# A tuned decoder layer on one core: one of the four weight-block sums of each gate/up group moves from VectorE to GpSimd

## The chip, the core and the metric

The kernel runs on one core of a Trainium2 chip. The core's engines each have an instruction queue of their own and work in parallel: TensorE (PE in the profile; its weight loads are PEld), VectorE (DVE), ScalarE (ACT), GpSimd (POOL) and SyncE (SP), which here only starts DMA transfers. An engine takes its queue strictly in order; semaphores tie the queues together. The metric is the device time of one execution in microseconds (us); the kernel before takes 2040.13 us, the median of two runs (2040.05 and 2040.21).

## The reference, cut to what matters

One decoder layer on 256 tokens of width 2048, all in float32. It has a SwiGLU feed-forward half-step, a token mixer of two attention branches, and a second SwiGLU half-step, each followed by a LayerNorm:

```python
def _swiglu(x, w_gate, w_up, w_down):
    return (jax.nn.silu(x @ w_gate) * (x @ w_up)) @ w_down

h = _layer_norm(ALPHA * h + 0.5 * _swiglu(h, ffn1_w_gate, ffn1_w_up, ffn1_w_down), ln1_g, ln1_b)
mix = _mixer(h, ...)
h = _layer_norm(ALPHA * h + mix, ln2_g, ln2_b)
h = _layer_norm(ALPHA * h + 0.5 * _swiglu(h, ffn2_w_gate, ffn2_w_up, ffn2_w_down), ln3_g, ln3_b)
```

Here x is 256 x 2048, and w_gate and w_up are each 2048 x 5632. The change touches only the products x @ w_gate and x @ w_up of the two half-steps.

## The kernel before, in words

**Products in three parts.** A float32 product is made of three TensorE products in the type fp32r. Every operand is split into a high part (a rounding cast on ScalarE, line 149) and a low part (operand minus high part, a two-input subtract on VectorE, line 150). `triple` issues high x high, high x low and low x high (lines 202, 203, 204); line 203 is the first to read the low part of a weight tile.

**The ring.** Weights come from memory in pieces of 128 x 1024 floats (512 KB), which SyncE fetches. The two halves of a split piece go into a pair of `wring` tiles; in this stage six pairs are used in turn. A piece is one unit of work: its load is issued, some units later its `prep` makes the split, some units later still `now` issues its matmuls. A pair is free again when TensorE has done with it, so ScalarE's cast for a later unit waits for TensorE when the ring is full.

**Groups.** The gate and up weights are laid out in chunks of 512 columns (256 gate, 256 up). The first two chunks of a half-step go the plain way (`project`). The other twenty are taken two by two: ten groups per half-step, 20 in all. In a group (`Hybrid.group`) the upper half of the depth is multiplied plainly (eight `plain` units of 12 matmuls, whose tiles are called `raw`), and the lower half by a scheme with seven block products in place of eight (`seventh`; 14 units of 6 matmuls, with activations called `xs`). The scheme multiplies sums of weight blocks. There are four blocks, "11", "12", "21" and "22", each of two pieces (s = 0 and 1), in eight fixed tiles called `sraw`: 451 and 452 hold block 11, 453 and 454 block 12, 455 and 456 block 21, 457 and 458 block 22, in the first half-step. Products 5, 6, 7 and 4 need a sum, made in place by VectorE in `prep` (line 316) just ahead of the split: for product 5 block 11 += block 12, for product 6 block 11 += block 22, for product 7 block 12 += block 22, for product 4 block 11 += block 21. That is eight adds of 128 x 1024 in a group and 160 in all. The products stand in the order 1, 5, 6, 7, 2, 4, 3, with a plain unit behind each.

**Other work of a group.** When a bank of sums is complete, VectorE adds a stored product (line 504) and multiplies gate and up (line 495), ScalarE applies the SiLU (line 491), VectorE transposes 32 x 32 blocks (line 483), and GpSimd starts eight DMAs that write the result to memory (line 485). These DMA starts are all that GpSimd does in the groups.

**What sets the order.** The program is not issued in the order of the code: a scheduler places every instruction into its engine's queue when the kernel is built. So an edit in one place can shift neighbours on other queues.

Of the kernel before, what the change touches and what calls it, by code (L numbers as in the profile page):

```python
# [15 lines left out]
ALU = mybir.AluOpType  # L16
# [43 lines left out]
def layer_kernel(ctx: ExitStack, tc: tile.TileContext, a: dict, out: bass.AP):  # L60
    nc = tc.nc
    V, S, GP, PE = nc.vector, nc.scalar, nc.gpsimd, nc.tensor
# [9 lines left out]
    def nm(s):  # L72
        uid[0] += 1
        return f"{s}_{uid[0]}"
# [10 lines left out]
    def mm_bank(name="mm"):  # L85
        return psum.tile([P, 512], F32, tag="mm", name=nm(name), bufs=5)
# [61 lines left out]
    def split(hi, lo, src):  # L148
        S.copy(hi, src)  # L149
        V.tensor_tensor(out=lo, in0=src, in1=hi.bitcast(F32), op=ALU.subtract)  # L150
# [12 lines left out]
    def catch_up(n):  # L163
        while len(behind) > n:
            behind.popleft()()
# [22 lines left out]
    def unit(load, prep, now, later_on=None):  # L188
        if load is not None:
            load()  # L190
        loaded.append((prep, now, later_on))
        advance(*ahead)

    def next_pair():
        assert len(ring) > len(prepared) + lag[0], (len(ring), len(prepared), lag[0])
        catch_up(len(ring) - 1)
        pair = ring.pop(0)
        ring.append(pair)
        return pair

    def triple(o, xh, xl, wh, wl, first, last, again=False):
        PE.matmul(o, xh, wh, start=first, stop=False, skip_group_check=again)  # L202
        PE.matmul(o, xh, wl, start=False, stop=False, skip_group_check=again)  # L203
        PE.matmul(o, xl, wh, start=False, stop=last, skip_group_check=again)  # L204
# [68 lines left out]
    class Hybrid:  # L273
# [8 lines left out]
        def group(self, w0, w1, done):  # L282
            banks = {}
            snap = [t[:, i, :] for t in self.snaps[self.turn % 2] for i in range(2)]
            self.turn += 1
            n1, n2, n3, q5 = snap
            R = self.raws
            blocks = {"11": (w0, 0), "12": (w1, 0), "21": (w0, 2), "22": (w1, 2)}

            plan = {1: ("11", "11", None, "X"), 5: ("12", "11", ("11", "12"), "Z"), 6: ("22", "11", ("11", "22"), "X"),  # L290
                    7: (None, "12", ("12", "22"), "X"), 2: ("21", "21", None, "Y"), 4: (None, "11", ("11", "21"), "W"),
                    3: (None, "22", None, "Z")}
            after = {1: lambda: S.copy(n1, banks["X"]), 6: lambda: S.copy(n2, banks["X"]),  # L293
                     7: lambda: S.copy(n3, banks["X"]), 5: lambda: S.copy(q5, banks["Z"]),
                     2: lambda: done(0, 0, banks["Y"], n1, ALU.subtract),
                     4: lambda: done(0, 1, banks["W"], n3, ALU.subtract)}
            stops = {1, 5, 6, 7, 2, 4}

            def bank(n):
                first = n not in banks  # L300
                if first:
                    banks[n] = mm_bank()
                return banks[n], first

            def seventh(p, s):
                load_block, src, add, b = plan[p]
                st = {}

                def load():
                    w, j0 = blocks[load_block]  # L310
                    nc.sync.dma_start(R[load_block][s], w[j0 + s])

                def prep():
                    t = R[src][s]
                    if add is not None:
                        V.tensor_tensor(out=t, in0=t, in1=R[add[1]][s], op=ALU.add)  # L316
                    pair = next_pair()
                    split(*pair, t)
                    st["pair"] = [v.rearrange("p (g n) -> p g n", g=G) for v in pair]

                def now():
                    o, first = bank(b)
                    wh, wl = st["pair"]
                    xh, xl = self.seven.at_[p]
                    for g in range(G):
                        k = 2 * s + g
                        triple(o, xh[:, k, :], xl[:, k, :], wh[:, g, :], wl[:, g, :], first and g == 0,
                               s == 1 and g == 1 and p in stops, b in "XZ")
                    if s == 1 and p in after:
                        after[p]()  # L330
                unit(load if load_block else None, prep, now)

            def plain(n, j, last=False):
                w = (w0, w1)[n]
                names = (("Y", "W"), ("Z", "X"))[n]
                st = {}

                def load():
                    st["raw"] = wpool.tile([P, 1024], F32, tag="raw", name=nm("raw"), bufs=4)
                    nc.sync.dma_start(st["raw"], w[j])  # L340

                def prep():
                    pair = next_pair()
                    split(*pair, st["raw"])
                    st["pair"] = [v.rearrange("p (g n) -> p g n", g=G) for v in pair]

                def now():
                    wh, wl = st["pair"]
                    for b in range(2):
                        o, first = bank(names[b])  # L350
                        for g in range(G):
                            k = 2 * j + g
                            triple(o, self.x.at(0, k, b), self.x.at(1, k, b), wh[:, g, :], wl[:, g, :],
                                   first and g == 0, last and g == 1, n == 1)
                    if last:
                        done(1, 0, banks["Z"], n2, ALU.add)
                        done(1, 1, banks["X"], q5, ALU.add)
                unit(load, prep, now)

            end = self.k_tiles // G - 1  # L360
            for p, n, j in ((1, 0, 4), (5, 0, 5), (6, 0, 6), (7, 0, 7), (2, 1, 4), (4, 1, 5), (3, 1, 6)):
                for s in range(2):
                    seventh(p, s)
                plain(n, j)
            plain(1, end, True)
# [642 lines left out]
```

## Time and profile before

| what | value |
|---|---|
| time, median of two runs | 2040.13 us |
| span of the profiled execution, first to last instruction | 2038.9 us |
| PE busy | 2016.2 us (99%) |
| DVE busy | 1513.5 us (74%) |
| ACT busy | 1153.0 us (57%) |
| POOL busy | 147.4 us (7%) |
| block sums on DVE (line 316) | 160, together 192.5 us, 1215 ns each |
| mean granted TensorE clock | 0.997 |

The profile gives no total of its own for its execution beside the span; the span is 1.2 us below the median of the runs. "Busy" is a share of the whole span, and the stages differ: the groups of the first half-step fill about 60 to 480 us of the span and those of the second about 1340 to 1790 us, and there VectorE is far busier than its 74%. A matmul's end is modelled, so a busy TensorE is best read by how many matmuls start in a stretch.

### The profile page before, as it was taken

How to read it: one execution, taken by the hardware profiler on the slowest of the kernel's cores; microseconds unless marked ns; L12 is line 12 of the kernel's file. 1: busy time of each engine (PE TensorE's matmuls, PEld its weight loads, DVE VectorE, ACT ScalarE, POOL GpSimd, SP SyncE). 2: the span in 40 equal slices, each digit the busy share in tenths (PEclk: the TensorE clock that was granted, in tenths of full speed). 3: DMA queues.
4: the chain of work that ended last, by engine and by line, in shares of the span. 5: the costliest groups of instructions: out<-in, count | busy, mean ns of one | idle time of the engine just before them, and what ended most of it. 6: DMA issues, size and time to landing. Idle time of an engine off the chain costs nothing.

```text
span 2038.9 us, 25040 instructions
## 1 busy us (share of the span) xinstructions
PE 2016.2 (99%) x9088; PEld 1668.6 (82%) x9088; DVE 1513.5 (74%) x1765; ACT 1153.0 (57%) x1443; POOL 147.4 (7%) x279
## 2 busy tenths in 40 slices
PE   8999999999999999999999999999999999999997
PEld 7788888887888888888888888878888888878886
DVE  6999999997545675455665555699999999965545
ACT  5666666675333565554674445476666666753332
POOL 0110001022000000000000000001000110220000
PEclk9999999999999999999999999999999999999999
DMA  7766766677655755544555575666676667785664
GB/s 268 250 202 221 247 217 196 217 274 272 203 193 192 237 183 199 171 150 155 166 170 192 187 277 187 214 230 222 215 238 227 198 214 237 246 290 193 196 194 136
DMA packets 123675, 432.15 MB, mean 212 GB/s; under 512 B 16464, under 2 KB 16544, under 8 KB 123552
## 3 DMA queue, kind: packets, MB, share of 16 engines
q1 hardware_dynamic: 108000, 387.50, 56.9%
q0 software_dynamic: 14400, 40.96, 6.4%
q10 hardware_dynamic: 1152, 2.10, 0.3%
q8 instruction: 71, 1.16, 0.2%
q14 instruction: 52, 0.43, 0.1%
HBM read 412.66 MB, written 17.83 MB: 211 GB/s over the span
## 4 chain that ended last, share of the span: by engine, by line
PE 90%; DVE 4%; DMA 3%; issue 3%; ACT 0%; POOL 0%; DVEq 0%; SPq 0%; ACTq 0%; POOLq 0%
PE mm L203 29%; PE mm L204 29%; PE mm L202 29%; DVE wring L150 2%; DMA sraw<-in_gu_dram 1%; DMA hraw<-hT 1%; DMA xraw<-in_xT_dram 1%; PE tr L370 1%; DVE sraw L316 1%; PE tr L652 0%; DMA raw<-in_gu_dram 0%; ACT wring L149 0%; PE tr L767 0%; PE tr L796 0%; PE tr L765 0%
## 5 line engine op out<-in xcount | busy, mean ns | idle before, releaser
L150 DVE TENSOR_TENSOR wring<-raw,wring 128x1024 fp32r<-128x1024 f32 (+1 forms) x582 | 702.7, 1210 | 433.5 <-ACT wring L149 428.7
L149 ACT CAST wring<-raw 128x1024 fp32r<-128x1024 f32 (+1 forms) x582 | 605.3, 1043 | 570.1 <-PE mm L204 489.0
L202 PE MATMUL mm<-wring,h 128*128 128x512 f32 (+2 forms) x1632 | 635.0, 389 | 1.6 <-ACT h L149 1.6
L204 PE MATMUL mm<-wring,h 128*128 128x512 f32 (+2 forms) x1632 | 630.3, 387 | 0.6 <-DVE h L150 0.6
L203 PE MATMUL mm<-wring,h 128*128 128x512 f32 (+2 forms) x1632 | 629.5, 386 | 0.8 <-DVE wring L150 0.8
L204 PEld LDWEIGHTS mm<-wring,h 128*128 128x128 f32 x1632 | 306.4, 188 | 63.7 <-DVE h L150 2.5
L202 PEld LDWEIGHTS mm<-wring,h 128*128 128x128 f32 x1632 | 306.6, 188 | 63.5 <-ACT h L149 3.4
L203 PEld LDWEIGHTS mm<-wring,h 128*128 128x128 f32 x1632 | 306.7, 188 | 61.9 <-DVE wring L150 2.1
L149 ACT CAST wring<-sraw 128x1024 fp32r<-128x1024 f32 x280 | 289.9, 1052 | 115.5 <-PE mm L204 74.6
L150 DVE TENSOR_TENSOR wring<-sraw,wring 128x1024 fp32r<-128x1024 f32 x280 | 335.7, 1219 | 9.3 <-ACT wring L149 6.8
L202 PE MATMUL mm<-wring,xs 128*128 128x512 f32 x560 | 218.0, 389 | 2.1 <-ACT snap L293 2.1
L203 PE MATMUL mm<-wring,xs 128*128 128x512 f32 x560 | 218.0, 389 | 0.5 <-DVE wring L150 0.5
L204 PE MATMUL mm<-wring,xs 128*128 128x512 f32 x560 | 217.9, 389 | 0.0
L316 DVE TENSOR_TENSOR sraw<-sraw,sraw 128x1024 f32<-128x1024 f32 x160 | 192.5, 1215 | 1.7 <-DMA sraw<-in_gu_dram 1.4
L202 PE MATMUL mm<-wring,x 128*128 128x512 f32 x384 | 149.6, 391 | 4.1 <-ACT x L149 4.1
L203 PE MATMUL mm<-wring,x 128*128 128x512 f32 x384 | 149.9, 391 | 0.8 <-DVE wring L150 0.8
L204 PE MATMUL mm<-wring,x 128*128 128x512 f32 x384 | 149.8, 391 | 0.0
L485 POOL DMA_DIRECT2D hT<-blocks x176 | 95.5, 550 | 665.6 <-DVE blocks L483 662.9
L202 PEld LDWEIGHTS mm<-wring,xs 128*128 128x128 f32 x560 | 105.1, 188 | 24.5 <-ACT snap L293 2.5
L203 PEld LDWEIGHTS mm<-wring,xs 128*128 128x128 f32 x560 | 105.1, 188 | 22.7 <-DVE wring L150 0.9
L204 PEld LDWEIGHTS mm<-wring,xs 128*128 128x128 f32 x560 | 105.1, 188 | 21.7
L202 PEld LDWEIGHTS mm<-wring,x 128*128 128x128 f32 x384 | 72.2, 188 | 19.9 <-ACT x L149 4.5
(239 smaller groups left out, 1543.1 us busy)
## 6 DMA issues: line engine op xcount, KB each, us to landing
raw<-in_gu_dram SPq DMA_DIRECT2D x192, 512.0 KB, 4.4
raw<-in_dn_dram SPq DMA_DIRECT2D x176, 512.0 KB, 3.4
sraw<-in_gu_dram SPq DMA_DIRECT2D x160, 512.0 KB, 5.3
raw<-in_wgm_dram SPq DMA_DIRECT2D x32, 512.0 KB, 3.4
raw<-in_wgd_dram SPq DMA_DIRECT2D x32, 512.0 KB, 3.3
raw<-in_w_out_dram SPq DMA_DIRECT2D x32, 512.0 KB, 3.5
hT<-blocks POOLq DMA_DIRECT2D x176, 64.0 KB, 2.5
hraw<-hT POOLq DMA_DIRECT2D x44, 256.0 KB, 5.0
```

The source lines that it names most:

```text
L149: S.copy(hi, src)
L150: V.tensor_tensor(out=lo, in0=src, in1=hi.bitcast(F32), op=ALU.subtract)
L202: PE.matmul(o, xh, wh, start=first, stop=False, skip_group_check=again)
L203: PE.matmul(o, xh, wl, start=False, stop=False, skip_group_check=again)
L204: PE.matmul(o, xl, wh, start=False, stop=last, skip_group_check=again)
L316: V.tensor_tensor(out=t, in0=t, in1=R[add[1]][s], op=ALU.add)
L370: PE.transpose(t[:, i * P:(i + 1) * P], src[:, i * P:(i + 1) * P], ident)
L485: nc.gpsimd.dma_start(hT[q, b].rearrange("(g r) (i f) -> i r g f", g=4, i=4)[i], t[32 * i:32 * (i + 1), :].rearrange("r (g f) -> r g f", g=4))
```

## The change

The two adds of product 7 (block 12 += block 22, s = 0 and 1) leave VectorE. GpSimd makes them, and they are issued in `prep` of product 6, beside the VectorE add of blocks 11 and 22, three units before the split that needs them. The arithmetic is the same. In each group VectorE has six adds of 128 x 1024 left and GpSimd gets two; over the kernel 40 adds move.

```diff
@@ -312,8 +312,10 @@
                 def prep():
                     t = R[src][s]
-                    if add is not None:
+                    if add is not None and p != 7:
                         V.tensor_tensor(out=t, in0=t, in1=R[add[1]][s], op=ALU.add)
+                    if p == 6:
+                        GP.tensor_tensor(out=R["12"][s], in0=R["12"][s], in1=R["22"][s], op=ALU.add)
                     pair = next_pair()
                     split(*pair, t)
```

Lines behind the edit have numbers higher by two in the changed kernel. The scheduler's order changes with it, shown here for the fifth and sixth groups of the first half-step.

VectorE's queue ahead of the transposes, before; `sraw_453` is block 12, piece 0:

```order
L316 TENSOR_TENSOR sraw_452<-sraw_452,sraw_454 128x1024
L150 TENSOR_TENSOR wring_107<-sraw_451,wring_106 128x1024
L316 TENSOR_TENSOR sraw_453<-sraw_453,sraw_457 128x1024
L504 TENSOR_TENSOR gus_2038<-mm_1804,snap_459 128x512
L150 TENSOR_TENSOR wring_125<-sraw_452,wring_124 128x1024
```

The same place now:

```order
L316 TENSOR_TENSOR sraw_452<-sraw_452,sraw_454 128x1024
L150 TENSOR_TENSOR wring_107<-sraw_451,wring_106 128x1024
L316 TENSOR_TENSOR sraw_451<-sraw_451,sraw_457 128x1024
L506 TENSOR_TENSOR gus_2038<-mm_1806,snap_459 128x512
L150 TENSOR_TENSOR wring_125<-sraw_452,wring_124 128x1024
```

The add of block 12's first piece is gone, and product 6's first add (block 11) has moved up into its place.

VectorE's queue behind the two transposes, before; it holds the splits of product 6 (`sraw_451`, `sraw_452`) and product 7 (`sraw_453`, `sraw_454`):

```order
L316 TENSOR_TENSOR sraw_451<-sraw_451,sraw_457 128x1024
L316 TENSOR_TENSOR sraw_452<-sraw_452,sraw_458 128x1024
L150 TENSOR_TENSOR wring_109<-raw_2071,wring_108 128x1024
L150 TENSOR_TENSOR wring_121<-sraw_451,wring_120 128x1024
L150 TENSOR_TENSOR wring_119<-sraw_452,wring_118 128x1024
L150 TENSOR_TENSOR wring_107<-sraw_453,wring_106 128x1024
L316 TENSOR_TENSOR sraw_454<-sraw_454,sraw_458 128x1024
L150 TENSOR_TENSOR wring_123<-raw_2109,wring_122 128x1024
L150 TENSOR_TENSOR wring_121<-sraw_455,wring_120 128x1024
L150 TENSOR_TENSOR wring_125<-sraw_454,wring_124 128x1024
```

The same place now:

```order
L150 TENSOR_TENSOR wring_121<-sraw_451,wring_120 128x1024
L316 TENSOR_TENSOR sraw_452<-sraw_452,sraw_458 128x1024
L150 TENSOR_TENSOR wring_109<-raw_2071,wring_108 128x1024
L316 TENSOR_TENSOR sraw_451<-sraw_451,sraw_455 128x1024
L150 TENSOR_TENSOR wring_119<-sraw_452,wring_118 128x1024
L150 TENSOR_TENSOR wring_107<-sraw_453,wring_106 128x1024
L150 TENSOR_TENSOR wring_125<-sraw_454,wring_124 128x1024
L150 TENSOR_TENSOR wring_123<-raw_2111,wring_122 128x1024
L150 TENSOR_TENSOR wring_121<-sraw_455,wring_120 128x1024
```

The add of block 12's second piece is gone; product 6's second split is still the fifth instruction behind the transposes, since product 4's first add (block 11 += block 21) has moved up ahead of it.

GpSimd's queue in this place now; before, it held only the line 485 rows:

```order
L318 TENSOR_TENSOR sraw_453<-sraw_453,sraw_457 128x1024
L318 TENSOR_TENSOR sraw_454<-sraw_454,sraw_458 128x1024
L487 DMA hT_132<-blocks_2059 32x4x128 x4
L487 DMA hT_132<-blocks_2065 32x4x128 x4
L318 TENSOR_TENSOR sraw_453<-sraw_453,sraw_457 128x1024
L318 TENSOR_TENSOR sraw_454<-sraw_454,sraw_458 128x1024
```

Each pair of adds stands ahead of the eight DMA starts that write the previous group's result.

## The prediction

> **What bounds the kernel now.** I read the page's busy times and its chain of waits first, then the table by stretch of time, then who waits for whom in the groups. First the two lines of the page, then two rows of the table by stretch:
>
> ```profile
> PE 2016.2 (99%) x9088; PEld 1668.6 (82%) x9088; DVE 1513.5 (74%) x1765; ACT 1153.0 (57%) x1443; POOL 147.4 (7%) x279
> PE 90%; DVE 4%; DMA 3%; issue 3%; ACT 0%; POOL 0%; DVEq 0%; SPq 0%; ACTq 0%; POOLq 0%
> ...
> core 0: us, PE busy (x) PEld busy (x) DVE busy (x) ACT busy (x) POOL busy (x), PEclk, DMA share, GB/s
> 270.30:311.10 40.80, 40.80 (x182) 33.80 (x181) 39.56 (x41) 26.38 (x30) 4.33 (x9) 1.00 0.66 219
> 1427.00:1467.80 40.80, 40.80 (x182) 33.78 (x181) 39.55 (x41) 26.38 (x32) 4.33 (x9) 1.00 0.67 219
> ```
>
> The chain is 90% TensorE. The two long rows are one group of each half-step. A group has 8 x 12 + 14 x 6 = 180 matmuls, and 40.8 us over 180 is 0.227 us each, at full clock and without a pause. Beside it VectorE is busy 39.56 of 40.8 us, so it has 1.2 us to spare in a group. TensorE binds, and VectorE follows close behind.
>
> ```profile
> PE mm L202 <- ACT snap L293: 2.1, 1, 2.1
> PE mm L204 <- DVE h L150: 0.6, 1, 0.6
> PE mm L203 <- DVE wring L150: 0.5, 1, 0.5
> PE mm L202 <- ACT h L149: 0.3, 1, 0.3
> ```
>
> These are all of TensorE's waits from 55 to 500 us (total, times, longest). The same view of 1310 to 1790 us has no row. So TensorE loses 3.5 us in the groups and around them, and nothing that is taken from VectorE there can bring more than that.
>
> How far is VectorE ahead of TensorE? The next fence shows one group's stretch: VectorE's timeline, then ScalarE's, then TensorE's (start, length, engine, line; in brackets the idle time before).
>
> ```profile
> 258.15 1.22 DVE L316 TENSOR_TENSOR sraw<-sraw,sraw 128x1024 f32<-128x1024 f32 x1
> ...
> 261.56 1.21 DVE L316 TENSOR_TENSOR sraw<-sraw,sraw 128x1024 f32<-128x1024 f32 x1
> 262.70 1.22 DVE L150 TENSOR_TENSOR wring<-sraw,wring 128x1024 fp32r<-128x1024 f32 x1
> 263.83 1.21 DVE L316 TENSOR_TENSOR sraw<-sraw,sraw 128x1024 f32<-128x1024 f32 x1
> 264.97 0.68 DVE L504 TENSOR_TENSOR gus<-mm,snap 128x512 f32<-128x512 f32 x1
> ...
> 269.11 1.30 DVE L483 STREAM_TRANSPOSE blocks<-hb 128x512 f32<-128x512 f32 x2
> 270.33 2.31 DVE L316 TENSOR_TENSOR sraw<-sraw,sraw 128x1024 f32<-128x1024 f32 x2
> 272.62 1.23 DVE L150 TENSOR_TENSOR wring<-raw,wring 128x1024 fp32r<-128x1024 f32 x1
> 273.76 3.49 DVE L150 TENSOR_TENSOR wring<-sraw,wring 128x1024 fp32r<-128x1024 f32 x3
> 277.17 1.22 DVE L316 TENSOR_TENSOR sraw<-sraw,sraw 128x1024 f32<-128x1024 f32 x1
> ...
> 263.37 1.05 ACT L149 CAST wring<-sraw 128x1024 fp32r<-128x1024 f32 x1 [1.67 <-PE mm L204]
> 271.53 1.06 ACT L149 CAST wring<-raw 128x1024 fp32r<-128x1024 f32 x1 [2.18 <-PE mm L204]
> 274.87 1.05 ACT L149 CAST wring<-sraw 128x1024 fp32r<-128x1024 f32 x1
> ...
> 276.96 0.39 PE L203 MATMUL mm<-wring,xs 128*128 128x512 f32 x1
> 278.32 0.39 PE L203 MATMUL mm<-wring,xs 128*128 128x512 f32 x1
> ```
>
> ScalarE's cast at 263.37 had waited 1.67 us for TensorE: the ring was full, and nothing could have been prepared earlier. From there VectorE works without a gap through adds, bank sums, transposes and splits, and its lead shrinks. The row at 273.76 holds three splits: product 6, pieces 0 and 1, and product 7, piece 0. Three in 3.49 us, each 1.22 long, start (3.49 - 1.22) / 2 = 1.14 us apart, so the second ends at 273.76 + 1.14 + 1.22 = 276.1. TensorE first reads its low part at 278.32. That is a lead of 2.2 us, the end of a burst, and it comes back in every group. **The cover over VectorE in this place is 2.2 us**, though it is idle 1.2 us per group elsewhere: idle time behind a full ring cannot be saved up.
>
> **The change part by part.**
>
> *What VectorE loses.* Two adds per group. Adds start 1.13 or 1.14 us after the instruction before (262.70 to 263.83, 263.83 to 264.97), so two are worth 2.3 us per group and 46 us over the 20. TensorE was not waiting for them, so by itself this gives between 0 and 3.5 us. I take 0.
>
> *Where it is lost.* The add at 263.83 (block 12, piece 0) goes, and product 6's first add takes its place. The one at 277.17 (piece 1) goes from behind the tight split. Ahead of that split stand as many VectorE instructions as before, because block 11 += block 21 has moved up. So the lead of 2.2 us there is not made larger by the saving.
>
> *What GpSimd gets.* Two adds of 128 x 1024, two tiles in, one out. Before has no such add; these are its nearest rows, three from GpSimd's groups by shape (count, then busy us and mean ns) and one from its timeline.
>
> ```profile
> L584 POOL TENSOR_SCALAR_AFFINE_SELECT mask<-mask 128x128 f32<-128x128 f32 x2 | 0.5, 287 | 0.0
> L582 POOL MEMSET mask<- 128x384 f32 x1 | 0.4, 422 | 0.0
> ...
> L992 POOL MEMSET const-float32-0.0<- 128x1 f32 x1 | 0.1, 98 | 0.2 <-issue 0.2
> ...
> 270.10 4.33 POOL L485 DMA_DIRECT2D hT<-blocks  x8 [36.47 <-DVE blocks L483]
> ```
>
> One element costs 98 ns, so 98 ns is the fixed part. A fill of 384 takes 422: (422 - 98) / 384 = 0.84 ns per element for one stream. The select reads one tile and writes one: (287 - 98) / 128 = 1.48 ns. An add has one more stream to read. Low: two streams at fill speed, 1024 x 1.69 + 98 = 1.83 us. Middle: select plus one stream, 1024 x 2.32 + 98 = 2.47 us. High: two selects, 1024 x 2.95 + 98 = 3.12 us. I take 2.3 us, near the middle.
>
> *Is GpSimd in time?* Its first add needs only the VectorE add of blocks 11 and 12 to be over (258.15 + 1.22 = 259.4), the second the one at 261.56 (262.8); block 22 has landed, since the add at 263.83 ran without a gap. The first user is the cast of block 12 at 274.87. Two adds of 2.3 us are done by about 265 to 267. They stand ahead of the eight DMA starts, which began at 270.10 when the transposes released them; these wait for nothing new, and what they write is read only at the end of the half-step. GpSimd has 36.47 us of idle time there, so the add's own length is hidden.
>
> *What the add does to VectorE.* This decides, and no row shows it: before never has GpSimd reading tiles beside VectorE. The bounds for the time that VectorE stands still per add are 0 and the whole add (3.12 us). The nearest row speaks for little: beside the DMA starts at 270.10 VectorE's adds run at (272.62 - 270.33) / 2 = 1.145 us instead of 1.135. But a DMA start reads no tile, and both the add and the VectorE instructions beside it stream two. I choose the upper kind, a VectorE that stands still for the whole add, 2.3 us.
>
> [...]
>
> *The sum.* Both adds fall between 259.4 and the tight split. VectorE reaches that split 2 x 2.3 = 4.6 us later, 2.2 of them are covered, and TensorE waits 2.4 us. Behind it VectorE has time enough (1.2 + 2.3 us saved) to fill the ring again by the next burst; so the loss comes anew in every group: 20 x 2.4 = 48 us. The profiled span of 2038.9 becomes 2087, and with the 1.2 us by which the median stands above it, **2088 us**, 2.3% slower. In short, with B for the standstill per add: loss = 20 x (2B - 2.2). B = 1.83 gives 29 us (2069), 3.12 gives 81 (2121), B up to 1.1 gives none.
>
> [...]
>
> *Small things.* ScalarE's queue gets one more table load near the first group. A table load takes 1.28 us in this row:
>
> ```profile
> 80.83 1.28 ACT L630 ACT_TABLE_LOAD   x1
> ```
>
> That is once, and it is the most it can cost. SyncE's loads keep their number; a few change places at the start of each half-step, for which I allow 2 us either way.
>
> **The rivals.**
>
> *The engines do not hold each other (0.26).* VectorE simply does 2.3 us less per group, TensorE keeps its 0.227 us per matmul, and the time is 2040 less 0 to 3.5 us: about 2038, not slower. The spacing of 1.145 us beside the DMA starts speaks for it. It decides whenever B stays below 1.1 us, since the lead of 2.2 us then covers both adds.
>
> *GpSimd only gets in where VectorE leaves room (0.18).* If VectorE's back-to-back instructions keep the add waiting, it starts at one that does not read two such tiles, as at 264.97 (0.6 us to the next), and VectorE stands still for 2.3 - 0.6 = 1.7 us: 20 x (3.4 - 2.2) = 24 us, 2064. If both go on at half pace, B is about 1.15 and the loss 2 us. So 2040 to 2064.
>
> *GpSimd comes too late (0.02).* If its adds wait so long that the second ends past the cast at 274.87, product 7's split is late too, and each microsecond costs another 20 us: above 2104.
>
> That the scheduler undoes the change can be excluded: the adds stand in GpSimd's queue, and VectorE's queue has two fewer.
>
> **How the numbers follow.** A measurement here can tell about 2%, 41 us; the mark is 2081, which is B = 2.13. The standstill for a whole add has 0.54: 0.46 with B above 2.13, 0.08 with a shorter add (2069 to 2081). The forecast is 2088. The range must take in the rival without contention, 2036, and at the top B = 2.7, 2104; outside lie longer adds and late ones, under 0.2. Slower by over 2%: 0.46 + 0.02 = 0.48. Within 2%: 0.08 + 0.18 + 0.26 = 0.52, less 0.01. Faster by over 2%: 0.01, since TensorE's waits leave 3.5 us to gain.
>
> **What would show it.** GpSimd has 40 adds, 2.3 us each. VectorE's spacing in those moments grows from 1.14 to over 3 us. TensorE gets waits for line 150, about 2.4 us per group, and a group grows from 40.8 to 43.2 us. Under the first rival the groups stay at 40.8 us and VectorE's busy time falls to about 37.3. Wrong in its core would be a group that stays at 40.8 us while VectorE stands still, or one that grows with GpSimd's adds late and VectorE free.

## The result and the profile after

The changed kernel takes 2112.75 us (median of two runs, 2110.06 and 2115.44) against 2040.13 us: a ratio of 1.0351, 95% interval 1.0333 to 1.0368, so 3.5% slower. The forecast was 2088 us and its range ended at 2104. The direction was right; of some 72 us the sum had 48. The profiled execution has a span of 2108.3 us, 69.4 us more than before, and a mean granted TensorE clock of 0.984 against 0.997.

The page of the changed kernel (lines below 318 have moved down by two) shows the moved work: busy times, chain, and the groups of the adds.

```profile
PE 2049.8 (97%) x9088; PEld 1684.0 (80%) x9088; DVE 1554.1 (74%) x1725; ACT 1146.8 (54%) x1444; POOL 281.5 (13%) x319
PE 86%; DVE 6%; issue 4%; DMA 3%; POOL 1%; ACT 1%; DVEq 0%; ACTq 0%; SPq 0%; POOLq 0%
...
L318 POOL TENSOR_TENSOR sraw<-sraw,sraw 128x1024 f32<-128x1024 f32 x40 | 134.1, 3352 | 542.7 <-DVE sraw L316 491.3
L316 DVE TENSOR_TENSOR sraw<-sraw,sraw 128x1024 f32<-128x1024 f32 x120 | 186.3, 1554 | 3.6 <-DMA sraw<-in_gu_dram 2.9
```

GpSimd has the 40 adds. VectorE has 40 instructions fewer, but is busy for 41 us more: its remaining adds last 1554 ns in the mean and not 1215 as before. The place to look at first is one group of the first half-step, in the timelines of GpSimd and VectorE (start, length, engine, line; in brackets the idle time before).

```profile
273.55 3.31 POOL L318 TENSOR_TENSOR sraw<-sraw,sraw 128x1024 f32<-128x1024 f32 x1 [25.34 <-DVE sraw L316]
279.16 3.31 POOL L318 TENSOR_TENSOR sraw<-sraw,sraw 128x1024 f32<-128x1024 f32 x1 [2.30 <-DVE sraw L316]
288.61 4.33 POOL L487 DMA_DIRECT2D hT<-blocks  x8 [6.14 <-DVE blocks L485]
```

```profile
273.39 1.22 DVE L150 TENSOR_TENSOR wring<-sraw,wring 128x1024 fp32r<-128x1024 f32 x1
274.52 3.42 DVE L150 TENSOR_TENSOR wring<-raw,wring 128x1024 fp32r<-128x1024 f32 x1
277.87 1.21 DVE L316 TENSOR_TENSOR sraw<-sraw,sraw 128x1024 f32<-128x1024 f32 x1
279.01 1.21 DVE L150 TENSOR_TENSOR wring<-sraw,wring 128x1024 fp32r<-128x1024 f32 x1
280.25 3.30 DVE L316 TENSOR_TENSOR sraw<-sraw,sraw 128x1024 f32<-128x1024 f32 x1
283.48 0.68 DVE L506 TENSOR_TENSOR gus<-mm,snap 128x512 f32<-128x512 f32 x1
```

Beside each of the two GpSimd adds exactly one VectorE instruction is long: 3.42 and 3.30 us in place of 1.22. So it is in the whole trace: 40 of VectorE's two-input instructions last over 1.6 us, one for each add (34 of them 3.3 to 3.4 us, the others 2.8 to 3.2); in the trace of the kernel before there is none. Start to start it is 277.87 - 274.52 = 3.35 and 283.48 - 280.25 = 3.23 us; without the add it would be 1.14. So VectorE stands still for **2.21 and 2.09 us**, 4.3 us in a group. GpSimd's own 3.31 us holds both a wait and the work: its first add is recorded from 273.55, but VectorE's split of 273.39 still ends in time (274.61); the work lies behind that, 276.86 - 274.61 = 2.25 us.

What TensorE makes of it is in its timeline, at product 6, second piece:

```profile
292.30 0.50 PE L202 MATMUL mm<-wring,xs 128*128 128x512 f32 x1
294.61 0.50 PE L203 MATMUL mm<-wring,xs 128*128 128x512 f32 x1 [1.81 <-DVE wring L150]
...
295.63 0.63 PE L203 MATMUL mm<-wring,xs 128*128 128x512 f32 x1
296.06 0.63 PE L204 MATMUL mm<-wring,xs 128*128 128x512 f32 x1
296.49 0.63 PE L202 MATMUL mm<-wring,x 128*128 128x512 f32 x1
...
298.59 0.40 PE L204 MATMUL mm<-wring,x 128*128 128x512 f32 x1
298.82 0.40 PE L202 MATMUL mm<-wring,x 128*128 128x512 f32 x1
```

There are two losses. The first is a pause: line 203 starts 2.31 us after line 202, not 0.23, because line 150 of VectorE is late. The second was not in the forecast: from 295.2 to 298.6 the matmuls start 0.43 us apart and not 0.23. The table by stretch (length; busy time of PE, PEld, DVE, ACT, POOL with counts; granted clock, DMA share, GB/s) shows the whole group and those moments:

```profile
289.40:334.10 44.70, 42.88 (x182) 34.81 (x181) 41.70 (x39) 25.93 (x30) 10.92 (x11) 0.96 0.60 202
...
296.00:297.00 1.00, 1.00 (x4) 0.74 (x3) 1.00 (x2) 0.28 (x1) 0.00 (x0) 0.50 0.02 8
297.00:298.00 1.00, 1.00 (x4) 0.80 (x3) 1.00 (x2) 1.00 (x2) 0.00 (x0) 0.50 0.92 270
298.00:299.00 1.00, 1.00 (x4) 0.79 (x4) 1.00 (x1) 0.25 (x1) 0.00 (x0) 0.73 0.88 295
299.00:300.00 1.00, 1.00 (x6) 0.80 (x6) 1.00 (x2) 0.00 (x0) 0.00 (x0) 1.00 0.87 324
```

A group that took 40.8 us takes 44.7 here, at a mean clock of 0.96, and behind the pause TensorE is granted **half its clock** for about three microseconds. TensorE's waits in the whole span are led by one row: total, times, longest.

```profile
PE mm L203 <- DVE wring L150: 37.4, 23, 2.3
```

Before, that row had 2.1 us. So some 35 of the 69 us are booked as waits for line 150; the rest had to be found.

### The profile page after: what moved, and what is told of

It is laid out like the page before. It is cut to its first block, busy times and chain, and to the rows that moved or that the text cites. A ratio compares the mean times of both kernels' runs of the same rounds, so it can differ in the third digit from the quotient of the medians.

```text
span 2108.3 us, 25175 instructions
## 1 busy us (share of the span) xinstructions
PE 2049.8 (97%) x9088; PEld 1684.0 (80%) x9088; DVE 1554.1 (74%) x1725; ACT 1146.8 (54%) x1444; POOL 281.5 (13%) x319
## 4 chain that ended last, share of the span: by engine, by line
PE 86%; DVE 6%; issue 4%; DMA 3%; POOL 1%; ACT 1%; DVEq 0%; ACTq 0%; SPq 0%; POOLq 0%
PE mm L203 28%; PE mm L204 28%; PE mm L202 27%; DVE wring L150 3%; DVE sraw L316 2%; DMA hraw<-hT 1%; DMA xraw<-in_xT_dram 1%; PE tr L372 1%; POOL hT L487 1%; ACT wring L149 0%; DMA sraw<-in_gu_dram 0%; PE tr L654 0%; DMA z<-res 0%; DMA row_i<-in_pos_row_dram 0%; DVE gus L506 0%
## 5 line engine op out<-in xcount | busy, mean ns | idle before, releaser
L150 DVE TENSOR_TENSOR wring<-raw,wring 128x1024 fp32r<-128x1024 f32 (+1 forms) x582 | 743.7, 1280 | 453.6 <-ACT wring L149 448.2
L203 PE MATMUL mm<-wring,xs 128*128 128x512 f32 x560 | 224.8, 401 | 36.0 <-DVE wring L150 36.0
L202 PE MATMUL mm<-wring,xs 128*128 128x512 f32 x560 | 222.6, 397 | 2.8 <-ACT snap L293 2.1
L204 PE MATMUL mm<-wring,xs 128*128 128x512 f32 x560 | 223.3, 399 | 0.0
L318 POOL TENSOR_TENSOR sraw<-sraw,sraw 128x1024 f32<-128x1024 f32 x40 | 134.1, 3352 | 542.7 <-DVE sraw L316 491.3
L316 DVE TENSOR_TENSOR sraw<-sraw,sraw 128x1024 f32<-128x1024 f32 x120 | 186.3, 1554 | 3.6 <-DMA sraw<-in_gu_dram 2.9
L203 PEld LDWEIGHTS mm<-wring,xs 128*128 128x128 f32 x560 | 106.9, 191 | 64.4 <-DVE wring L150 42.6
L202 PE MATMUL mm<-wring,x 128*128 128x512 f32 x384 | 153.0, 400 | 4.1 <-ACT x L149 4.1
L203 PE MATMUL mm<-wring,x 128*128 128x512 f32 x384 | 152.7, 399 | 0.8 <-DVE wring L150 0.8
L204 PE MATMUL mm<-wring,x 128*128 128x512 f32 x384 | 152.0, 397 | 0.0
L202 PEld LDWEIGHTS mm<-wring,xs 128*128 128x128 f32 x560 | 106.2, 190 | 31.6 <-ACT wring L149 7.6
L204 PEld LDWEIGHTS mm<-wring,xs 128*128 128x128 f32 x560 | 107.7, 192 | 21.7
```

Source lines behind the costliest of these rows:

```text
L318: GP.tensor_tensor(out=R["12"][s], in0=R["12"][s], in1=R["22"][s], op=ALU.add)
```

## The experiments

The theory after the first look had two parts: a GpSimd add that reads tiles holds VectorE for its whole length (2.2 us), and the pause of TensorE that follows makes its clock fall. The rivals were that the new order of VectorE's and SyncE's queues costs something by itself; that the tiles or the writes are what collide; and that the clock falls for another reason (GpSimd's activity, or simply more of everything). Edits are shown against the changed kernel.

### The new order without GpSimd's add: drop

The GpSimd add is left out, so product 7 is computed without its sum.

```diff
-                    if p == 6:
-                        GP.tensor_tensor(out=R["12"][s], in0=R["12"][s], in1=R["22"][s], op=ALU.add)
```

> Product 7 goes without its sum: neither VectorE nor GpSimd makes the 40 adds (a part of the computation is left out), and VectorE's queue is the one of the changed kernel. Theory of the standstill (GpSimd's add keeps VectorE's two-input instructions waiting): with no add on GpSimd nothing stands still, groups of 40.8 us, TensorE without waits, about 2037 us (2040 less 0 to 3.5). Rival, the new order of VectorE's queue is what costs: the loss of 70 us stays, about 2110.

Measured: 2038.68 us (2036.97 to 2039.59), ratio 0.9989 (0.9979 to 0.9998). One group by stretch:

```profile
267.70:308.50 40.80, 40.80 (x182) 33.80 (x181) 37.43 (x39) 26.43 (x30) 4.34 (x8) 1.00 0.67 219
```

VectorE is busy for 37.43 us where it was 39.56, and the group still takes 40.80. VectorE's instructions stand in the order of the changed kernel, so the reordering costs nothing, and the saving on VectorE is worth 0.1%: so much the change would bring if GpSimd's adds cost nothing.

### One add of the two: one

```diff
-                    if add is not None and p != 7:
+                    if add is not None and (p != 7 or s == 1):
...
-                    if p == 6:
+                    if p == 6 and s == 0:
```

> GpSimd adds only piece 0 of block 12, VectorE keeps piece 1. Theory of the standstill behind a lead: VectorE stands still once per group, 2.2 us, and the lead of 2.0 to 2.2 us at product 6's splits covers it: a wait of TensorE of 0 to 0.2 us, 2040 to 2048. Rival, a loss in proportion to the adds that moved: half of 72 us, about 2076.

Measured: 2052.67 us (2050.96 to 2055.67), ratio 1.0062 (1.0047 to 1.0077). VectorE has one long instruction per group, and TensorE's row for line 150 is small:

```profile
264.54 3.42 DVE L150 TENSOR_TENSOR wring<-raw,wring 128x1024 fp32r<-128x1024 f32 x1
267.88 1.21 DVE L316 TENSOR_TENSOR sraw<-sraw,sraw 128x1024 f32<-128x1024 f32 x1
```

```profile
PE mm L203 <- DVE wring L150: 4.8, 10, 1.0
```

The hold is 267.88 - 264.54 - 1.14 = 2.2 us, as much as TensorE's lead of 2.0 to 2.2, and the group grows only by 0.37 us (41.17). Half of the adds cost 12.5 of 72 us. So the loss is not proportional to the adds: the lead pays for the first, the second goes straight to TensorE. That is what the term with the lead says. The time is still 5 us above the expected 2048: the groups account for 20 x 0.37 = 7.4 us, and the trace has two windows of half clock more than before (one at 20 us, one at 78 us; their price, up to 1.6 us each, is worked out below). The last 2 us were not followed.

### Which part of the add holds VectorE: copy and memset

In copy, GpSimd copies block 22 over block 12 (one tile in, one out); in memset it fills the tile three times (none in, one out). Both leave product 7's sum out.

```diff
-                        GP.tensor_tensor(out=R["12"][s], in0=R["12"][s], in1=R["22"][s], op=ALU.add)
+                        GP.tensor_copy(R["12"][s], R["22"][s])
```

```diff
-                        GP.tensor_tensor(out=R["12"][s], in0=R["12"][s], in1=R["22"][s], op=ALU.add)
+                        for _ in range(3):
+                            GP.memset(R["12"][s], 0.01)
```

> In place of each add GpSimd copies block 22's piece over block 12's (one tile read, one written; the sum is left out). If reading one tile is enough to hold VectorE: a standstill of the copy's length, which by the select and fill rows is 1.0 to 1.6 us per piece, seen as VectorE instructions of 2.2 to 2.8 us; twice that against the lead of 2.2 gives a TensorE wait of 0 to 1 us per group, with the slower clock behind it 2037 to 2090. If it takes two read streams: VectorE stays at 1.22 us each, about 2037.

> In place of each of GpSimd's adds stand three fills of the same tile (they write and read nothing; the sum is left out). By the fill rows of before a fill of 1024 takes 0.96 us, three 2.9 us, longer than the add held VectorE (2.2 us). Theory that only GpSimd's reading of tiles holds VectorE: no standstill, VectorE keeps its spacing of 1.14 us, groups of 40.8 us, about 2037. Rival, any GpSimd access to the tiles holds it: 2.9 us per piece, more than in the changed kernel, over 2120.

Measured: copy 2041.12 us (2039.82 to 2041.63), ratio 1.0003 (0.9993 to 1.0012); memset 2038.58 us (2037.23 to 2040.98), ratio 0.9992 (0.9982 to 1.0001). First copy's timelines, GpSimd then VectorE:

```profile
259.46 1.98 POOL L318 COPY sraw<-sraw 128x1024 f32<-128x1024 f32 x1 [24.12 <-DVE sraw L316]
...
260.45 2.06 DVE L150 TENSOR_TENSOR wring<-raw,wring 128x1024 fp32r<-128x1024 f32 x1
262.43 1.21 DVE L316 TENSOR_TENSOR sraw<-sraw,sraw 128x1024 f32<-128x1024 f32 x1
```

VectorE's instruction beside the copy takes 262.43 - 260.45 = 1.98 us start to start, a hold of 0.84. Two of them are 1.7 us, less than the lead of 2.2, and TensorE sees nothing. Now memset, GpSimd then VectorE:

```profile
257.53 2.99 POOL L319 MEMSET sraw<- 128x1024 f32 x3 [25.66 <-DVE sraw L316]
...
257.39 1.22 DVE L150 TENSOR_TENSOR wring<-sraw,wring 128x1024 fp32r<-128x1024 f32 x1
258.52 1.22 DVE L150 TENSOR_TENSOR wring<-raw,wring 128x1024 fp32r<-128x1024 f32 x1
259.66 1.22 DVE L316 TENSOR_TENSOR sraw<-sraw,sraw 128x1024 f32<-128x1024 f32 x1
```

Here GpSimd writes for 3 us beside three VectorE instructions of two inputs, and each has its usual 1.22 us; in the whole trace, with 120 fills, no two-input instruction of VectorE lasts over 1.6 us. The instructions of VectorE have the same order in both runs as in the changed kernel. So in these runs GpSimd's reading holds VectorE (0.84 us beside the copy, which reads one tile, 2.1 to 2.2 beside the add, which reads two), and its writing alone does not (0 beside the fills).

### Spare work in the pause, with and without the change: fill_after and fill_before

Nine spare matmuls of 512 columns (2.0 us) go ahead of product 6's second piece, into the place of TensorE's pause; their result is not used. fill_after is the changed kernel with them, fill_before the kernel before.

```diff
                 def now():
...
+                    if p == 6 and s == 1:
+                        spare = tr_bank()
+                        for _ in range(9):
+                            PE.matmul(spare, xh[:, 2, :], wh[:, 0, :], start=True, stop=True)
```

> The changed kernel with nine added matmuls of 512 columns per group on TensorE, ahead of product 6's second piece, where TensorE waits; their result is used by nothing. If the lower clock behind the wait comes from TensorE's idle time: the nine take 2.04 us, about as long as the wait, TensorE does not fall idle, the clock stays at 1.0, and a group takes 40.8 + 2.1 = 42.9 us: about 2084, faster than the changed kernel by 28 although it does more. If the clock drops for another reason (GpSimd's work, say), they come on top or change nothing: 2112 to 2150.

> The kernel before with the same nine added matmuls per group. TensorE was never waiting there: 180 matmuls of 2.04 us per nine more, 20 x 2.04 = 41 us, about 2081, under every theory. It is the measure for the run above: if that one is within 5 us of this one, the standstill is wholly hidden under the added matmuls.

Measured: fill_after 2097.10 us (2096.20 to 2101.18), ratio 1.0282 (1.0266 to 1.0297); fill_before 2081.75 us (2080.22 to 2084.05), ratio 1.0203 (1.0186 to 1.0220). On the kernel before, 20 x 9 matmuls cost 41.6 us, their 20 x 9 x 0.227 = 41 us. On the changed kernel the same work **saves** 15.6 us. A pause that is merely filled could at best cost nothing; the saving is the clock, which is 0.996 here in place of 0.984. It was above the expected 2084 by 13 us: a shorter wait for line 150 was left (5.6 us in all), and the groups take 43.14 us. It is also 15 us above fill_before, not within the 5 that were named, so the hold is not wholly hidden: a group takes 42.84 us there, which makes 6 of the 15.

### Less spare work: fill4 and fill2

The same edit with four matmuls (0.91 us) and with two (0.45 us).

> The changed kernel with four added matmuls per group (0.9 us) where TensorE waits, not nine. They do not lengthen a group as long as they fit into the wait; about 1.2 us of idle time is left. If so short a wait still halves the clock: 44.7 us per group, about 2112. If it does not: 40.8 + 2.1 = 42.9 us per group, 2090 to 2098, clock back near 0.997.

> The changed kernel with two spare matmuls (0.45 us) on TensorE ahead of product 6, piece 1; the sum of each wait and the spare work stays 2.3 us. Theory (a window that idles for more than about 0.6 of 3.413 us): the idle time is then at most about 1.9 us, 0.55 of a window, so no window is slow, the clock is 0.997 and the time that of four spare matmuls, 2093 us (2091 to 2096). Rival (the slow time falls off with the wait by degrees): half-way between no spare matmul and four, about 2103 us, clock about 0.990.

Measured: fill4 2092.89 us (2091.58 to 2093.34), ratio 1.0257 (1.0239 to 1.0275), clock 0.997; fill2 2094.05 us (2091.04 to 2094.51), ratio 1.0267 (1.0251 to 1.0282), clock 0.996. TensorE's row for line 150 in fill4 and, below, in fill2:

```profile
PE mm L203 <- DVE wring L150: 22.9, 25, 1.8
```

```profile
PE mm L203 <- DVE wring L150: 30.2, 26, 1.9
```

Pause and spare work together are still 2.2 us in a group (2.3 in the changed kernel), so next to nothing of the wait is won; yet both kernels are 19 to 20 us faster than the changed one, and as fast as each other. So the slow clock is worth about 20 us, and it does not shrink by degrees with the pause: half a microsecond less in the pause takes nearly all of it away. GpSimd's 40 adds run in both, so their activity alone does not lower the clock.

### The same VectorE time without GpSimd: late

GpSimd's add is left out, product 7 goes without its sum, and VectorE repeats product 6's own sum (once in full, twice on half the columns).

```diff
-                        GP.tensor_tensor(out=R["12"][s], in0=R["12"][s], in1=R["22"][s], op=ALU.add)
+                        n = (1024, 512)[s]
+                        for _ in range(1 + s):
+                            V.tensor_tensor(out=t[:, 0:n], in0=t[:, 0:n], in1=R["22"][s][:, 0:n], op=ALU.add)
```

> No add on GpSimd. Product 7's sum is left out; in its place VectorE repeats product 6's own sum, once more for piece 0 and twice on half the columns for piece 1 (the result is wrong by that), so that the low part of product 6's second piece comes about 4.6 us later than before, as in the changed kernel, while VectorE's total work is that of before. Theory that TensorE's clock falls because TensorE had to wait: a wait of 2.1 to 2.4 us per group, behind it half clock for about 3 us as in the changed kernel, a group of about 45 us, 2110 to 2125 us. Rival, the clock falls because of GpSimd's work: only the wait is lost, 20 x 2.4 = 48 us, about 2088, mean clock 0.997.

Measured: 2045.87 us (2044.42 to 2047.38), ratio 1.0027 (1.0016 to 1.0038). A miss: there was no such pause. TensorE's timeline at product 6 shows why; the last row is VectorE's, and product 6's second split is the first of its two.

```profile
279.55 0.39 PE L204 MATMUL mm<-wring,x 128*128 128x512 f32 x1
279.78 0.39 PE L202 MATMUL mm<-wring,x 128*128 128x512 f32 x1
280.04 0.50 PE L202 MATMUL mm<-wring,xs 128*128 128x512 f32 x1
280.38 0.39 PE L203 MATMUL mm<-wring,x 128*128 128x512 f32 x1
...
282.00 0.39 PE L203 MATMUL mm<-wring,xs 128*128 128x512 f32 x1
...
280.58 2.35 DVE L150 TENSOR_TENSOR wring<-sraw,wring 128x1024 fp32r<-128x1024 f32 x2
```

Here a product with `xs` is begun in the middle of a triple with `x`, and seven matmuls with `x` stand between its lines 202 (280.04) and 203 (282.00). The scheduler lays out TensorE's queue when the kernel is built, and it knew of the longer VectorE work: it put other matmuls into the gap. The delay itself was there: product 6's second split ends at 280.58 + 1.21 = 281.79, 11.5 us behind the start of the transposes against 7.0 in the kernel before. So late is no test of the clock. It shows something else: a split that comes 4.6 us later costs 7 us here, against drop, where the scheduler sees why, and over 50 in the changed kernel, where it doesn't. The two are not wholly alike: in late VectorE's added work is 2.2 us in a group (busy 1515.1 us against drop's 1471.5), in the changed kernel the holds are 4.3.

### A second trace, and a shift behind the pause: after_again and shift5

The changed kernel's first trace has 15 waits of 2.31 or 2.32 us within its groups. Behind 11 of them comes a slow stretch, behind 4 none (at 204, 382, 1512 and 1689 us). Neither the wait's length nor its place in the group tells them apart. A grid does. In the trace's record of the granted clock, from which the PEclk column is made, every stretch of half clock in the groups is 3.413 us long (once twice that), and their starts lie whole multiples of 3.413 us apart: those at 250.76, 295.13 and 339.50 us, say, 13 windows from one to the next. How long TensorE idles in a window is counted here by taking a matmul to occupy 0.227 us (0.427 at half clock) from its start, which are the median distances between starts in that trace from 55 us on. The next fence has two windows and the two behind them, from the changed kernel, within 0.04 us of that grid:

```profile
core 0: us, PE busy (x) PEld busy (x) DVE busy (x) ACT busy (x) POOL busy (x), PEclk, DMA share, GB/s
291.75:295.16 3.41, 1.59 (x6) 0.85 (x5) 3.41 (x4) 3.41 (x5) 1.19 (x3) 1.00 0.79 231
295.16:298.58 3.42, 3.42 (x9) 2.63 (x8) 3.42 (x4) 1.93 (x3) 0.00 (x0) 0.51 0.47 149
380.49:383.90 3.41, 1.80 (x7) 0.95 (x6) 3.41 (x4) 3.22 (x4) 1.94 (x4) 1.00 0.74 161
383.90:387.31 3.41, 3.21 (x14) 2.69 (x15) 3.41 (x4) 2.70 (x4) 0.00 (x0) 1.00 0.56 197
```

In the first, with six matmuls, TensorE idles for 0.68 of the window, and the next is at half clock. In the third, the same wait reaches 0.2 us across the edge; seven matmuls are in the window, it idles for 0.58, and the next is at full clock. Two runs were to test that: the changed kernel again, without an edit, and one with five spare matmuls **behind** the pause, which leave the pause alone but make a group's length nearly 13 windows.

```diff
                                s == 1 and g == 1 and p in stops, b in "XZ")
+                    if p == 6 and s == 1:
+                        spare = tr_bank()
+                        for _ in range(5):
+                            PE.matmul(spare, xh[:, 2, :], wh[:, 0, :], start=True, stop=True)
                     if s == 1 and p in after:
```

> The changed kernel once more, with nothing edited, for a second trace. Theory (a fixed grid): TensorE's clock is decided on a grid of 3.413 us that runs on its own; where TensorE idles for more than about 0.6 of one such window, the next window runs at clock 0.50. In the first trace of the changed kernel 13 of the 18 waits of 2.3 us within the groups were followed by such a window, each costing about 1.6 us. Here the waits stay at 2.3 us and some 12 to 15 of them, not all, are followed by a slow stretch of up to 3.4 us, whose ends lie again on a grid of 3.413 us (another phase); time 2110 to 2116 us. Rival (the length of the wait alone decides): all waits of 2.3 us would be followed by a slow stretch, or none.

> The changed kernel with five spare matmuls (1.13 us) on TensorE right behind product 6, piece 1, that is behind the wait: the wait stays 2.3 us, and a group without a slow window takes 43.13 + 1.13 = 44.26 us, nearly 13 windows of 3.413 us (44.37). Theory (fixed grid): a wait that once straddles two windows does so in the next group too (it moves by only 0.11 us), while a slow window moves the next wait by 1.5 us; so of the 18 to 20 waits at most some 5 are followed by slow clock: 2093 + 20 x 1.13 = 2116 us, plus up to 8: 2116 to 2124 us, clock above 0.992. Rival (each wait of 2.3 us is as likely as before to be followed by slow clock, wherever it lies): 2113 + 23 = 2136 us, clock about 0.984.

Measured: after_again 2111.41 us (2109.43 to 2114.28), ratio 1.0354 (1.0337 to 1.0371), clock 0.984; shift5 2118.12 us (2115.60 to 2121.03), ratio 1.0388 (1.0373 to 1.0404), clock 0.992. In after_again 12 of 15 waits of 2.3 us had a slow stretch behind them, on a grid of the same 3.413 us. In shift5, by the same count, it was **3 of 15** (behind the waits that end at 164.63, 431.90 and 1479.58 us). One such wait in shift5, with full clock at once behind it, in TensorE's timeline:

```profile
252.50 0.50 PE L202 MATMUL mm<-wring,xs 128*128 128x512 f32 x1
254.82 0.50 PE L203 MATMUL mm<-wring,xs 128*128 128x512 f32 x1 [1.82 <-DVE wring L150]
255.16 0.40 PE L204 MATMUL mm<-wring,xs 128*128 128x512 f32 x1
255.40 0.39 PE L202 MATMUL mm<-wring,xs 128*128 128x512 f32 x1
```

The wait is as long as in the changed kernel (2.32 us). With 20 x 1.13 = 22.7 us more work shift5 is only 5 to 7 us slower than the two runs of the changed kernel, where a fixed loss behind each wait would give 2136. So in these three runs it is where the wait lies on the grid that decides.

That the clock falls without GpSimd's adds too is in the trace of the kernel before. Its two longest pauses behind the first 3 us, on the grid that its one slow stretch gives (the stretch ends at 20.94 us):

```profile
14.12:17.54 3.42, 0.75 (x3) 0.67 (x4) 0.69 (x1) 1.42 (x3) 0.00 (x0) 1.00 1.05 399
17.54:20.95 3.41, 3.41 (x9) 2.64 (x9) 3.14 (x5) 3.41 (x8) 0.00 (x0) 0.50 0.31 123
72.15:75.56 3.41, 2.92 (x13) 2.07 (x12) 2.66 (x10) 0.00 (x0) 0.00 (x0) 1.00 0.85 341
75.56:78.97 3.41, 1.80 (x8) 1.50 (x9) 1.67 (x3) 2.95 (x4) 0.00 (x0) 1.00 1.00 405
```

The first window idles for 0.82 of its length and a window at clock 0.50 follows. The pause at 75 us (2.49 us from start to start) is split over two windows, neither of which idles for more than 0.51, and the clock stays at 1.00.

## Why the prediction was right and wrong

**TensorE binds; what VectorE saves is worth 0 to 3.5 us.** Right: drop has the saving alone and gains 1.5 to 2 us.

**The lead of 2.2 us.** Nearly right. A hold of 2.2 us per group costs 0.37 us (one), holds of 1.7 cost nothing (copy), and 4.3 us cost TensorE 2.3. By these costs the lead is 1.8 to 2.0 us.

**The length of the add, 2.3 us, and a VectorE that stands still for all of it.** Right: 2.21 and 2.09 us. That VectorE stands still for the whole add was the author's choice between two bounds; the trace of the kernel before has no GpSimd add to read it from. Of the three rows that bounded the add, the middle one was the good one. GpSimd's instructions measure 3.35 us in the mean, not 2.3, since the record includes the wait for VectorE; "40 adds, 2.3 us each" was wrong as a thing to look for.

**The rivals.** That the engines do not hold each other falls with the two long VectorE instructions per group. That GpSimd only gets in where VectorE leaves room falls as well: its add got in between two back-to-back instructions with two inputs each. It was not late: its second add is over at 282.47, and its DMA starts at 288.61 still waited for VectorE's transposes. The order of VectorE's and SyncE's queues costs nothing (drop).

**The sum: "loss = 20 x (2B - 2.2)".** This is the step that failed. As a sum of TensorE's waits it was nearly exact: a group with the pause and without slow clock takes 43.13 us in fill4 (248.69 to 291.82), and the changed kernel's own group without a slow window takes 43.12 (378.10 to 421.22 between its DMA starts); 43.13 - 40.80 = 2.33 us, times 20 is 47 us, against 48. But the formula prices TensorE's pause at the pause, and behind most pauses there is a second price, half clock, for which the sum had no term. A window of 3.413 us at half clock holds 3.413 / 0.427 = 8 matmuls and not 15; it costs 7 x 0.227 = 1.6 us. The groups show it: 44.73 us (288.61 to 333.34) with a slow window, 43.12 without. There are 15 slow windows from the groups on in the trace of the changed kernel, at most 15 x 1.6 = 24 us; that trace is 2108.3 - 2089.6 = 18.7 us longer than fill4's, and the medians differ by 19.9. About 47 and 20 of the 72 us are so accounted for. The remaining 5 seem to lie outside the groups' regular stretch: fill4, without slow windows there, loses 2.9 us up to its first DMA starts (65.29 us against 62.36) and 4.3 us between the half-steps' groups. That is somewhat more than what remains, so other places give a little back; why was not followed.

**The waits "about 2.4 us per group, and a group grows from 40.8 to 43.2 us".** The wait was right; 43.2 is right for the groups whose pause lies well on the grid, and 44.7 is what most of them take. The range ended at 2104 because it was made of bounds for B alone. A term for what a pause does to TensorE behind it was nowhere in it, though the row of the kernel before at 18 to 21 us (clock 0.50 behind a 4 us pause) stood in the trace that was read.

**What is shown and what is argued.** Shown: the hold, by reading and not by writing; the lead; that shortening the pauses takes nearly all of the slow clock away; that a shift behind the pause takes most of it away with the pause left in. Read from the traces, not set by an edit: the window's length, from the record of the granted clock, and the idle share at which the clock falls, from the starts of the matmuls. Not shown: a pause of 2.3 us in the groups that comes from VectorE's own work; late did not make one.

## What to carry to other kernels

Moving a two-input sum from VectorE to GpSimd lost time here, where VectorE's other instructions read two tiles too: VectorE stood still for about as long as GpSimd worked, 2.2 us, to save 1.14. Price a pause of the bounding engine by what follows it as well: here a 2.3 us wait cost 3.9 us where it filled most of a clock window, and 0.9 us of useless matmuls in it won 20 us. And a delay that the scheduler foresees can be far cheaper than one that it doesn't: in late it filled the gap with other work.

## What the runs showed of the hardware that was not expected

- **The clock fell on a grid of 3.413 us.** In the traces of all thirteen runs shown here, from 55 us on and up to the last 4 us, 36 full-clock windows of the grid idled for 0.63 or more, and all were followed by a window at 0.50. Of the nine that idled for 0.586 to 0.62, four were, and of all that idled for less, none. One slow window that idled for a quarter was followed by a second slow one (at 1828 us in the first trace of the changed kernel). The grid's place differs from run to run (the two traces of the changed kernel have it at different places); what that adds to the spread of the times was not tested.
- **Less than a whole idle window was enough.** The waits in the groups of the two traces of the changed kernel were shorter than the grid's 3.413 us (2.3 us from start to start for most, 3.2 at the longest), and behind windows that idled for about 0.6 of their length the clock was 0.50 all the same.
- **The hold depended on the reads.** At 128 x 1024, a GpSimd add (two tiles read) held VectorE for 2.1 to 2.2 us, a copy (one) for 0.84, and a fill (none) not at all, though three fills take 3 us.
